# Dropping tokens over capacity: a whole-array copy moved from two DMA queues to one, with the drop test rebuilt on raw semaphores

## The chip, the core and the metric

The kernel runs on one core of one Trainium2 chip. The metric is device time in microseconds (us), lower is better. The time of the kernel before is the median of three runs; beside it stands one profiled execution, which gives the span from the first to the last instruction and everything that is read from the trace. TensorE's granted clock was 1.000 in it.

## What is computed

```python
batch, seq, hidden, capacity = 16, 1024, 512, 256
x = randn(batch, seq, hidden)                            # float32
token_positions = randint(0, capacity, (batch, seq))     # int64 on the device

mask = token_positions < capacity
return x * mask[..., None]
```

There are 16,384 rows of 512 float32 numbers, 2 KB a row and 33.55 MB in all. A row whose position is at or above the capacity becomes zero; any other row is copied. The positions are drawn below the capacity, so with these inputs every row is kept and the output equals x. The kernel doesn't rely on that: it tests the positions while it runs.

## The kernel before, in words

The kernel bets that most rows are kept. It copies all of x to the output from memory to memory, works out a mask meanwhile, and repairs the parts that hold a dropped row.

**The copy (L75).** The rows are seen as 128 groups of 128 neighbouring rows (`(p n) d -> p n d`); a group is 256 KB. The copy is cut along the row in the group into four transfers `k` of 32 rows each (`FIX_COLS`), so that a transfer has 128 pieces of 64 KB, 256 KB apart. Transfers 0 and 2 are issued by SyncE (SP), 1 and 3 by ScalarE (ACT), each with its own DMA queue. They stand at the head of both queues, but for the load of the positions, which SP issues first (L57).

**The mask (L60 to L115).** The positions come as 16 rows of 8 KB. Each is a 64-bit integer, so it is seen as a low and a high 32-bit half: VectorE (DVE) converts `lo` (L81) and `hi` (L82) to float32, makes four comparisons (L86 to L98), and joins them to `f_tile` (L101 to L103): kept if the high half is zero and the low half in 0 to capacity, or if the high half is negative. This mask lies on 16 partitions. To bring it to the 128 partitions of the copy, GpSimd (POOL) builds a selection matrix `e_all` (L60 to L65), and TensorE (PE) multiplies the two in eight steps into `m_psum` (L107), which DVE copies to `m_tile` (L115).

**The flags (L118 to L134).** DVE sums the mask over each of the four parts (`red`), PE sums over the partitions (`s_psum`, L124), and DVE compares with the number of rows in a part: `flag_i` holds four numbers, 1 where a row of the part is dropped. SP, ACT and DVE load all four into registers (L137 and the two lists after it).

**The repair (L153 to L183).** POOL fills two buffers `xt_z` of 8 MB with zeros. For each part u, a load of x into a buffer, 32 multiplications by columns of the mask under a branch on DVE, and a store to the output follow. The load (L163) and the store (L183) are conditional transfers: each is issued in any case and skipped by the value of its flag. The framework's scheduler places the semaphore waits: a store to a part of the output waits until the copy of that part has landed, also when the store is going to be skipped.

```python
eng.dma_start(out=out_r[:, f0 : f0 + FIX_COLS, :], in_=xt,
              cond=eng_flags[eng][u], cond_hint=False)
```

The order on the queues is the order of the code: on SP the positions, copies 0 and 2, loads 0 and 1, stores 1 and 2; on ACT copies 1 and 3, store 0, loads 2 and 3, store 3.

Of the kernel before, what the change touches and what calls it, by code (L numbers as in the profile page):

```python
# [8 lines left out]
@with_exitstack  # L9
def kernel(  # L10
    ctx: ExitStack,
    tc: tile.TileContext,
    x: bass.AP,
    token_positions: bass.AP,
    capacity: bass.AP,
    out: bass.AP,
):
    nc = tc.nc
    P = nc.NUM_PARTITIONS
    fp32 = mybir.dt.float32  # L20
    i32 = mybir.dt.int32

    x_f = x.flatten_outer_dims()
    out_f = out.flatten_outer_dims()
    N, D = x_f.shape
    assert N % P == 0
    n_per_p = N // P

    x_r = x_f.rearrange("(p n) d -> p n d", p=P)
    out_r = out_f.rearrange("(p n) d -> p n d", p=P)  # L30

    tp_f = token_positions.flatten_outer_dims()
    tp_r = tp_f.rearrange("b s -> (b s)") if len(tp_f.shape) == 2 else tp_f
    tp_i32 = tp_r.bitcast(mybir.dt.int32)
    QP = 16
    G = P // QP
    tp_pn = tp_i32.rearrange("(q w) -> q w", q=QP)

    cap = float(int(capacity))

    FIX_COLS = 32
    assert n_per_p % FIX_COLS == 0
    n_fix = n_per_p // FIX_COLS
    rows_per_fix = P * FIX_COLS

    sp = nc.sync
    act = nc.scalar
    hw = (sp, act)

    mask_pool = ctx.enter_context(tc.tile_pool(name="mask", bufs=1))  # L50
    psum_pool = ctx.enter_context(tc.tile_pool(name="psum", bufs=1, space=bass.MemoryType.PSUM))
    NBUF = 2
    io_pool = ctx.enter_context(tc.tile_pool(name="io", bufs=1))

    rows_q = N // QP
    tp_tile = mask_pool.tile([QP, rows_q * 2], i32)
    sp.dma_start(out=tp_tile, in_=tp_pn)  # L57

    e_iota = mask_pool.tile([QP, P], i32, name="e_iota")
    nc.gpsimd.iota(e_iota, pattern=[[1, P]], base=0, channel_multiplier=-G)  # L60
    e_iota_f = mask_pool.tile([QP, P], fp32, name="e_iota_f")
    nc.gpsimd.tensor_copy(out=e_iota_f, in_=e_iota)  # L62
    e_all = mask_pool.tile([QP, G, P], fp32, name="e_all")
    for b in range(G):
        nc.gpsimd.tensor_scalar(  # L65
            out=e_all[:, b, :],
            in0=e_iota_f,
            scalar1=float(b),
            scalar2=None,
            op0=mybir.AluOpType.is_equal,  # L70
        )

    for k in range(n_fix):
        c0 = k * FIX_COLS
        hw[k % 2].dma_start(  # L75
            out=out_r[:, c0 : c0 + FIX_COLS, :], in_=x_r[:, c0 : c0 + FIX_COLS, :]
        )

    lo = mask_pool.tile([QP, G, P], fp32)
    hi = mask_pool.tile([QP, G, P], fp32)  # L80
    nc.vector.tensor_copy(out=lo, in_=tp_tile[:, 0 : 2 * rows_q : 2])  # L81
    nc.vector.tensor_copy(out=hi, in_=tp_tile[:, 1 : 2 * rows_q : 2])  # L82

    f_tile = mask_pool.tile([QP, G, P], fp32)
    t_hi = mask_pool.tile([QP, G, P], fp32)
    nc.vector.tensor_scalar(  # L86
        out=t_hi, in0=hi, scalar1=0.0, scalar2=None, op0=mybir.AluOpType.is_equal
    )
    m2 = mask_pool.tile([QP, G, P], fp32)
    nc.vector.tensor_scalar(  # L90
        out=m2, in0=lo, scalar1=cap, scalar2=None, op0=mybir.AluOpType.is_lt
    )
    m3 = mask_pool.tile([QP, G, P], fp32)
    nc.vector.tensor_scalar(  # L94
        out=m3, in0=lo, scalar1=0.0, scalar2=None, op0=mybir.AluOpType.is_ge
    )
    t_neg = mask_pool.tile([QP, G, P], fp32)
    nc.vector.tensor_scalar(  # L98
        out=t_neg, in0=hi, scalar1=0.0, scalar2=None, op0=mybir.AluOpType.is_lt
    )  # L100
    nc.vector.tensor_tensor(out=f_tile, in0=t_hi, in1=m2, op=mybir.AluOpType.mult)  # L101
    nc.vector.tensor_tensor(out=f_tile, in0=f_tile, in1=m3, op=mybir.AluOpType.mult)  # L102
    nc.vector.tensor_tensor(out=f_tile, in0=f_tile, in1=t_neg, op=mybir.AluOpType.add)  # L103

    m_psum = psum_pool.tile([P, P], fp32, space=bass.MemoryType.PSUM, name="m_psum")
    for b in range(G):
        nc.tensor.matmul(  # L107
            out=m_psum,
            lhsT=e_all[:, b, :],
            rhs=f_tile[:, b, :],  # L110
            start=(b == 0),
            stop=(b == G - 1),
        )
    m_tile = mask_pool.tile([P, n_fix, FIX_COLS], fp32)
    nc.vector.tensor_copy(out=m_tile, in_=m_psum)  # L115

    red = mask_pool.tile([P, n_fix], fp32)
    nc.vector.tensor_reduce(  # L118
        out=red, in_=m_tile, axis=mybir.AxisListType.X, op=mybir.AluOpType.add
    )  # L120
    ones = mask_pool.tile([P, 1], fp32)
    nc.vector.memset(ones, 1.0)  # L122
    s_psum = psum_pool.tile([1, n_fix], fp32, space=bass.MemoryType.PSUM)
    nc.tensor.matmul(out=s_psum, lhsT=ones, rhs=red, start=True, stop=True)  # L124
    flag_f = mask_pool.tile([1, n_fix], fp32)
    nc.vector.tensor_scalar(  # L126
        out=flag_f,
        in0=s_psum,
        scalar1=float(rows_per_fix) - 0.5,
        scalar2=None,  # L130
        op0=mybir.AluOpType.is_lt,
    )
    flag_i = mask_pool.tile([1, n_fix], i32)
    nc.vector.tensor_copy(out=flag_i, in_=flag_f)  # L134

    sp_flags = [
        sp.value_load(flag_i[0:1, u : u + 1], min_val=0, max_val=1)  # L137
        for u in range(n_fix)
    ]
    act_flags = [  # L140
        act.value_load(flag_i[0:1, u : u + 1], min_val=0, max_val=1)
        for u in range(n_fix)
    ]
    ve_flags = [
        nc.vector.value_load(flag_i[0:1, u : u + 1], min_val=0, max_val=1)
        for u in range(n_fix)
    ]
    eng_flags = {sp: sp_flags, act: act_flags}

    xts = []  # L150
    for b in range(NBUF):
        zt = io_pool.tile([P, FIX_COLS, D], fp32, name=f"xt_z{b}")
        nc.gpsimd.memset(zt, 0.0)  # L153
        xts.append(zt)

    ld_eng = {0: sp, 1: sp, 2: act, 3: act}
    st_eng = {0: act, 1: sp, 2: sp, 3: act}

    def emit_load_and_mul(u):
        f0 = u * FIX_COLS  # L160
        xt = xts[u % NBUF]
        eng = ld_eng[u]
        eng.dma_start(  # L163
            out=xt,
            in_=x_r[:, f0 : f0 + FIX_COLS, :],
            cond=eng_flags[eng][u],
            cond_hint=False,
        )
        with tc.If(ve_flags[u]):
            for j in range(FIX_COLS):  # L170
                nc.vector.tensor_scalar(
                    out=xt[:, j, :],
                    in0=xt[:, j, :],
                    scalar1=m_tile[:, u, j : j + 1],
                    scalar2=None,
                    op0=mybir.AluOpType.mult,
                )

    def emit_store(u):
        f0 = u * FIX_COLS  # L180
        xt = xts[u % NBUF]
        eng = st_eng[u]
        eng.dma_start(  # L183
            out=out_r[:, f0 : f0 + FIX_COLS, :],
            in_=xt,
            cond=eng_flags[eng][u],
            cond_hint=False,
        )

    emit_load_and_mul(0)  # L190
    emit_load_and_mul(1)
    emit_store(0)
    emit_store(1)
    emit_load_and_mul(2)
    emit_load_and_mul(3)
    emit_store(2)
    emit_store(3)


# [1 line left out]
_INS = ['x', 'token_positions', 'capacity']  # L201
_OUTS = [((16, 1024, 512), 'float32')]
#: Inputs that are plain numbers.
_NUMBERS = {'capacity': 256}


# [26 lines left out]
```

## Time and profile before

| What | Value |
|---|---|
| median of 3 runs | 106.83 us (106.81 to 107.74) |
| span of the profiled execution | 104.9 us |
| instructions in it | 202 |
| DVE busy | 46.6 us |
| POOL busy | 50.7 us |
| PE busy | 3.9 us |
| bytes moved by DMA packets | 33.69 MB |
| longest DVE instruction (L81, `lo`) | 25.1 us |
| POOL's two zero fills (L153) | 14.0 us each |

The profiled execution has no time of its own beside its span; the median lies 1.9 us above the span. To read the profile: PE is TensorE, DVE VectorE, ACT ScalarE, POOL GpSimd, SP SyncE; a `q` after an engine's name is its instruction queue, which issues transfers and waits. Queue q1 carries SP's transfers and q10 ACT's. The DMA row shows in tenths how busy the 16 DMA engines were in each of 40 slices of the span. In the answers by windows, a row is a stretch of time with each engine's busy time, the clock, the share of the DMA engines and the GB/s; a packet counts in the window in which it starts. The HBM line of the page comes from counters of transfers and not from the packets.

### The profile page before, as it was taken

What the parts mean: (1) busy time and instruction counts of PE and PEld (TensorE: products, weight loads), DVE (VectorE), ACT (ScalarE), POOL (GpSimd) and SP (SyncE); (2) the same over time, 40 slices, a digit from 0 to 9 for tenths busy, and PEclk for the clock granted to TensorE, in tenths of its full rate; (3) what the DMA queues carried; (4) which work ended last, traced back from release to release, by engine and by line L of the source; (5) the groups of instructions that cost most, each with busy time, mean ns of one, the idle gap of its engine ahead of it and who ended that gap; (6) DMA issues with size and microseconds to landing.
All of it is one profiled execution on the core that took longest, in us unless ns stands there. A gap on an engine that the chain in (4) does not pass through costs nothing.

```text
span 104.9 us, 202 instructions
## 1 busy us (share of the span) xinstructions
PE 3.9 (4%) x18; PEld 3.6 (3%) x18; DVE 46.6 (44%) x14; POOL 50.7 (48%) x16
## 2 busy tenths in 40 slices
PE   0000000000000000000940000000000000000000
PEld 0000000000000000000920000000000000000000
DVE  0599999999999999998030000000000000000000
POOL 7999999999999999999600000000000000000000
DMA  9299999909999939999919999759999929999930
GB/s 375 100 375 400 400 400 375 400 25 400 400 400 375 300 125 400 400 400 375 375 50 400 400 400 403 225 175 400 400 400 375 325 100 400 400 400 375 300 125 0
DMA packets 609, 33.69 MB, mean 321 GB/s; under 512 B 80, under 2 KB 80, under 8 KB 80
## 3 DMA queue, kind: packets, MB, share of 16 engines
q1 hardware_dynamic: 320, 16.91, 48.5%
q10 hardware_dynamic: 288, 16.78, 47.4%
q14 instruction: 1, 0.01, 0.0%
HBM read 67.24 MB, written 67.11 MB: 1281 GB/s over the span
## 4 chain that ended last, share of the span: by engine, by line
DVE 44%; PE 4%; DMA 3%; issue 0%
DVE lo L81 24%; DVE m L90 14%; PE m_psum L107 4%; DMA tp_tile<-in_token_positions_dram 3%; DVE f_tile L103 1%; DVE f_tile L102 1%; DVE f_tile L101 1%; DVE m L94 1%; DVE t_neg L98 1%; DVE t_hi L86 1%; DVE hi L82 1%; DVE m_tile L115 0%; DVE red L118 0%; PE s_psum L124 0%; DVE flag_f L126 0%
## 5 line engine op out<-in xcount | busy, mean ns | idle before, releaser
L153 POOL MEMSET xt_z<- 128x16384 f32 x2 | 28.0, 14012 | 0.0
L81 DVE CAST lo<-tp_tile 16x1024 f32<-16x1024 int32 x1 | 25.1, 25121 | 2.9 <-DMA tp_tile<-in_token_positions_dram 2.9
L62 POOL CAST e_iota_f<-e_iota 16x128 f32<-16x128 int32 x1 | 14.3, 14328 | 0.0
L90 DVE TENSOR_SCALAR m<-lo 16x1024 f32<-16x1024 f32 x1 | 14.3, 14305 | 0.0
L65 POOL TENSOR_SCALAR e_all<-e_iota_f 16x128 f32<-16x128 f32 x8 | 8.1, 1023 | 0.3
L107 PE MATMUL m_psum<-f_tile,e_all 16*128 16x128 f32 x16 | 3.8, 424 | 49.6 <-DVE f_tile L103 49.6
L107 PEld LDWEIGHTS m_psum<-f_tile,e_all 16*128 16x128 f32 x16 | 3.5, 326 | 49.6 <-POOL e_all L65 49.6
L115 DVE COPY m_tile<-m_psum 128x128 f32<-128x128 f32 x1 | 0.3, 292 | 3.9 <-PE m_psum L107 3.9
L103 DVE TENSOR_TENSOR f_tile<-f_tile,t_neg 16x1024 f32<-16x1024 f32 x1 | 1.2, 1211 | 0.0
L102 DVE TENSOR_TENSOR f_tile<-f_tile,m 16x1024 f32<-16x1024 f32 x1 | 1.2, 1211 | 0.0
L101 DVE TENSOR_TENSOR f_tile<-t_hi,m 16x1024 f32<-16x1024 f32 x1 | 1.2, 1204 | 0.0
L82 DVE CAST hi<-tp_tile 16x1024 f32<-16x1024 int32 x1 | 0.8, 760 | 0.0
L86 DVE TENSOR_SCALAR t_hi<-hi 16x1024 f32<-16x1024 f32 x1 | 0.8, 759 | 0.0
L94 DVE TENSOR_SCALAR m<-lo 16x1024 f32<-16x1024 f32 x1 | 0.8, 759 | 0.0
L98 DVE TENSOR_SCALAR t_neg<-hi 16x1024 f32<-16x1024 f32 x1 | 0.8, 759 | 0.0
L122 DVE MEMSET ones<- 128x1 f32 x1 | 0.1, 59 | 0.8 <-PEq L214 0.8
L60 POOL IOTA e_iota<- 16x128 int32 x1 | 0.2, 224 | 0.4 <-POOLq L214 0.4
L118 DVE TENSOR_REDUCE red<-m_tile 128x4 f32<-128x128 f32 x1 | 0.3, 286 | 0.0
L126 DVE TENSOR_SCALAR flag_f<-s_psum 1x4 f32<-1x4 f32 x1 | 0.1, 148 | 0.3 <-PE s_psum L124 0.3
L124 PE MATMUL s_psum<-red,ones 128*1 128x4 f32 x2 | 0.2, 166 | 0.7 <-DVE red L118 0.7
L214 POOL MEMSET const-float32-0.0<- 128x1 f32 x1 | 0.1, 98 | 0.2 <-issue 0.2
L134 DVE CAST flag_i<-flag_f 1x4 int32<-1x4 f32 x1 | 0.2, 156 | 0.0
(4 smaller groups left out, 0.4 us busy)
## 6 DMA issues: line engine op xcount, KB each, us to landing
tp_tile<-in_token_positions_dram SPq DMA_DIRECT2D x1, 128.0 KB
out_dram<-in_x_dram ACTq DMA_DIRECT2D x2
out_dram<-in_x_dram SPq DMA_DIRECT2D x2
xt_z<-in_x_dram SPq DMA_DIRECT2D x2
out_dram<-xt_z ACTq DMA_DIRECT2D x2
xt_z<-in_x_dram ACTq DMA_DIRECT2D x2
out_dram<-xt_z SPq DMA_DIRECT2D x2
```

The costliest lines, as they stand in the source:

```text
L62: nc.gpsimd.tensor_copy(out=e_iota_f, in_=e_iota)
L65: nc.gpsimd.tensor_scalar(out=e_all[:, b, :], in0=e_iota_f, scalar1=float(b), scalar2=None, op0=mybir.AluOpType.is_equal,)
L81: nc.vector.tensor_copy(out=lo, in_=tp_tile[:, 0 : 2 * rows_q : 2])
L82: nc.vector.tensor_copy(out=hi, in_=tp_tile[:, 1 : 2 * rows_q : 2])
L86: nc.vector.tensor_scalar(out=t_hi, in0=hi, scalar1=0.0, scalar2=None, op0=mybir.AluOpType.is_equal)
L90: nc.vector.tensor_scalar(out=m2, in0=lo, scalar1=cap, scalar2=None, op0=mybir.AluOpType.is_lt)
L94: nc.vector.tensor_scalar(out=m3, in0=lo, scalar1=0.0, scalar2=None, op0=mybir.AluOpType.is_ge)
L101: nc.vector.tensor_tensor(out=f_tile, in0=t_hi, in1=m2, op=mybir.AluOpType.mult)
L102: nc.vector.tensor_tensor(out=f_tile, in0=f_tile, in1=m3, op=mybir.AluOpType.mult)
L103: nc.vector.tensor_tensor(out=f_tile, in0=f_tile, in1=t_neg, op=mybir.AluOpType.add)
L107: nc.tensor.matmul(out=m_psum, lhsT=e_all[:, b, :], rhs=f_tile[:, b, :], start=(b == 0), stop=(b == G - 1),)
L153: nc.gpsimd.memset(zt, 0.0)
```

## The change

The function's body is written anew inside one critical section, where the scheduler places no waits; seven kinds of raw semaphores order the work.

- The copy is issued by SP alone. x is seen as 16 rows of 2 MB (`(e c) -> e c`), and nine transfers walk along these rows: 64 KB of each row, then 192 KB, then seven times 256 KB. All nine come first on SP's queue.
- The positions are loaded by ACT, as 128 rows of 1 KB, so that the mask lies on 128 partitions from the start. The selection matrix, its matmuls and POOL's part go.
- The mask takes four DVE operations straight on the integer halves (`ge`, `lt`, `low`, `keep`), a sum over the row (`kept`), one matmul over the partitions (`total`) and a comparison, which writes a single flag `drop_i`. Each waits for the one ahead by the semaphore `s_ve`.
- SP, ACT and DVE wait for the flag, load it into a register, and branch once. The repair, inside the branch, handles parts of 16 rows of each group in two buffers with ordinary transfers. ACT waits there for the whole copy before its first store. No zero fill is left.
- At the end SP waits until all nine transfers have landed.

The core of the new code (buffers, semaphores and unused helpers left out; the old code, which is printed above, is removed in full):

```diff
+        x_e = x_b.rearrange("(e c) -> e c", e=16)
+        out_e = out_b.rearrange("(e c) -> e c", e=16)
+        c = 64 * KB
+        at = 0
+        for n in [1, 3] + [4] * 7:
+            sp.dma_start(
+                out=out_e[:, at : at + n * c], in_=x_e[:, at : at + n * c]
+            ).then_inc(s_copy, 16)
+            at += n * c
+            n_copy += 1
...
+        act.dma_start(out=tp, in_=tp_i32.rearrange("(p w) -> p w", p=P)).then_inc(s_tp, 16)
+        lo = tp[:, 0 : 2 * n_per_p : 2]
+        hi = tp[:, 1 : 2 * n_per_p : 2]
...
+        ve.memset(ones, 1.0).then_inc(s_ve, 1)
+        ve.wait_ge(s_tp, 16)
+        ve.tensor_scalar(
+            out=ge, in0=lo, scalar1=0.0, scalar2=None, op0=Alu.is_ge
+        ).then_inc(s_ve, 1)
+        ve.wait_ge(s_ve, 2)
+        ve.scalar_tensor_tensor(
+            out=lt, in0=lo, scalar=cap, in1=ge, op0=Alu.is_lt, op1=Alu.mult
+        ).then_inc(s_ve, 1)
...
+        ve.wait_ge(s_ve, 5)
+        ve.tensor_reduce(
+            out=kept, in_=keep, axis=mybir.AxisListType.X, op=Alu.add
+        ).then_inc(s_ve, 1)
+        pe.wait_ge(s_ve, 6)
+        pe.matmul(out=total, lhsT=ones, rhs=kept, start=True, stop=True).then_inc(s_pe, 1)
+        ve.wait_ge(s_pe, 1)
+        ve.tensor_scalar(
+            out=drop_i, in0=total, scalar1=float(N) - 0.5, scalar2=None, op0=Alu.is_lt
+        ).then_inc(s_ve, 1)
...
+        for e in (sp, act, ve):
+            e.wait_ge(s_ve, 7)
+        ET = mybir.EngineType
+        drop = nc.values_load(
+            drop_i[0:1, 0:1],
+            engines=[ET.SP, ET.Activation, ET.DVE],
...
+        with nc.If(drop):
+            for u in range(n_fix):
+                b = u % NBUF
+                if u >= NBUF:
+                    sp.wait_ge(s_st[b], 16 * (u // NBUF))
+                sp.dma_start(out=xts[b], in_=x_r[:, u * F : (u + 1) * F, :]).then_inc(s_ld[b], 16)
+                ve.wait_ge(s_ld[b], 16 * (u // NBUF + 1))
...
+                if u == 0:
+                    act.wait_ge(s_copy, 16 * n_copy)
+                act.wait_ge(s_mul, (u + 1) * F)
+                act.dma_start(out=out_r[:, u * F : (u + 1) * F, :], in_=xts[b]).then_inc(s_st[b], 16)
...
+        sp.wait_ge(s_copy, 16 * n_copy)
```

## The prediction, made blind

> **What bounds the kernel now.** I read the page's slices and queues first, then the chain of waits, then the queues' own waits and timeline, and last the DMA column of the windows. All durations are of one profiled execution: span 104.9 us. The median of the three timed runs is 106.83, so 1.9 us lie outside the span; I keep them and make the sum as a difference from 106.83.
>
> The page, engines and queues:
>
> ```profile
> PE 3.9 (4%) x18; PEld 3.6 (3%) x18; DVE 46.6 (44%) x14; POOL 50.7 (48%) x16
> ...
> DMA  9299999909999939999919999759999929999930
> ...
> DMA packets 609, 33.69 MB, mean 321 GB/s; under 512 B 80, under 2 KB 80, under 8 KB 80
> ...
> q1 hardware_dynamic: 320, 16.91, 48.5%
> q10 hardware_dynamic: 288, 16.78, 47.4%
> ...
> HBM read 67.24 MB, written 67.11 MB: 1281 GB/s over the span
> ```
>
> The compute engines are idle for more than half of the span; the two queues together fill 95.9% of 16 engines' time. The 33.69 MB are x once (33.55) and the positions (0.13). So no row is dropped and the eight conditional transfers move nothing; the HBM line must count them as if they ran, for it has twice x. The packets can be counted: 80 small ones are 16 completions for each of five transfers. Of the other 528, 512 are the copy (32 per engine, 64 KB each) and 16 are the positions, one row per engine.
>
> The chain of waits ends at the drop flag, not at the kernel's end:
>
> ```profile
> 54.51 0.16 DVE flag_i L134
> ```
>
> The SP queue's own waits, then its timeline:
>
> ```profile
> SPq L137 <- DVE flag_i L134: 52.2, 1, 52.2
> SPq L183 <- DMA out_dram<-in_x_dram: 44.5, 2, 41.7
> ```
>
> ```profile
> 0.74 0.42 SPq L57 DMA_DIRECT2D tp_tile<-in_token_positions_dram  x1
> 1.22 1.26 SPq L75 DMA_DIRECT2D out_dram<-in_x_dram  x2
> 57.42 0.46 SPq L163 DMA_DIRECT2D xt_z<-in_x_dram  x2
> 58.60 45.07 SPq L183 DMA_DIRECT2D out_dram<-xt_z  x2
> ```
>
> The flag is known at 54.7, and SP then waits to about 103.5 for the copy (its last two issues' entry runs to 103.67). So the kernel is one 33.55 MB copy from memory to memory; the flag has 48 us to spare.
>
> The windows tell the pace, because they put a packet's bytes where it starts (the last two columns are DMA share and GB/s):
>
> ```profile
> 2.20:2.30 0.10, 0.00 (x0) 0.00 (x0) 0.00 (x0) 0.10 (x1) 1.00 8.14 2867
> 2.90:5.00 2.10, 0.00 (x0) 0.00 (x0) 1.23 (x1) 2.10 (x1) 1.00 0.00 0
> 5.10:5.20 0.10, 0.00 (x0) 0.00 (x0) 0.10 (x1) 0.10 (x1) 1.00 1.82 655
> 5.80:8.00 2.20, 0.00 (x0) 0.00 (x0) 2.20 (x1) 2.20 (x1) 1.00 0.00 0
> 8.00:8.10 0.10, 0.00 (x0) 0.00 (x0) 0.10 (x1) 0.10 (x1) 1.00 1.86 655
> 11.00:11.10 0.10, 0.00 (x0) 0.00 (x0) 0.10 (x1) 0.10 (x1) 1.00 4.11 1311
> 55.10:55.20 0.10, 0.00 (x0) 0.00 (x0) 0.00 (x0) 0.00 (x0) 1.00 2.09 655
> 64.90:65.00 0.10, 0.00 (x0) 0.00 (x0) 0.00 (x0) 0.00 (x0) 1.00 2.00 737
> 99.10:99.20 0.10, 0.00 (x0) 0.00 (x0) 0.00 (x0) 0.00 (x0) 1.00 2.30 655
> ```
>
> All 16 engines start a 64 KB packet at nearly the same time, then none starts until the next round; the "holes" in the DMA row are this beat against slices of 2.6 us, not idle time. Rounds 0 to 3 start at 2.2, 5.1, 8.0 and 11.0: 8.8 / 3 = 2.93 us each. The last of 32 starts at 99.1: (99.1 - 11.0) / 28 = 3.146 us each after the start. The engines are never idle, so only a faster round makes this kernel faster. A round reads 1.05 MB and writes 1.05 MB: 2.10 MB / 3.146 us = 667 GB/s at the memory, 716 in the first three rounds.
>
> **The change, part by part.**
>
> *Selection matrix, mask arithmetic, memsets of 14.0 us each, conditional transfers: removed.* POOL's 50.7 us and nearly all of DVE's 46.6 go. They all lie beside the copy; gain 0. The new flag: positions by ACT, then five DVE operations of 128 x 128, a one-column matmul and a comparison. By the row of the 128 x 128 copy (292 ns) the five take 1.5 us; even at the longest DVE row here (25.1 us, beside POOL's own slow work) the flag stands before the old one plus the positions' delay. That delay: ACT's eight 1 KB packets per engine may each have to let a 64 KB packet of the copy pass, 8 x 3.1 = 25 us. So the flag comes between 6 and 60 us. The copy covers that to 103; cost 0. If the cover were gone, all of it would count. One value load per engine for four, and one branch not taken: before, 54.7 to 57.4 for the same; hidden too.
>
> *SP's order.* Nine copy issues come first. Before, a 128-row issue took 0.58 to 0.64 us and the 16-row one 0.42, so nine take 3.8 to 5.8 us, over by 6.6 at the latest. The first holds one packet per engine (2.9 us of work), and the second is issued 0.4 to 0.6 us later, so no engine runs dry. Behind SP's new waits stand only its own load, branch and final wait; behind ACT's and DVE's only theirs. If a queue takes fewer descriptors at once (before, each had 18 per engine; now 41), SP stands in an issue, with nothing late behind it.
>
> *Start.* The positions were issued at 0.74 and their packets started from about 1.85; the copy started at 2.2. The copy's first packets should now start at about 1.85: gain up to 0.4. The positions' bytes then run within the copy: the same 0.4 us per engine if bytes count, up to 8 x 0.4 = 3.2 us if each 1 KB packet costs as much as 8 KB did (ten packets in 1.8 to 2.1, by their share 0.38 us each). I take bytes, since semaphore packets of 4 B leave no gap in the rounds. Net 0, from -0.4 to +2.8.
>
> *End.* Before, SP is released at about 103.5 and the span ends at 104.9. A skipped store of 0.1 us goes, the end of the critical section comes; SP's waits at the kernel's own ends sum to 0.6 us. From -0.1 to +0.6; I take 0.
>
> *The copy itself.* This decides. Before, an engine's 32 packets come from two queues and jump by 256 KB; now they are 32 neighbours by address in one 2 MB block, from one queue. Sixteen rows do reach 16 engines: the 16-row positions transfer gave 16 completions. Whether engine and block were differently matched before, the views don't show. No row is this pattern. The nearest rows are both in this trace: 3.146 us per round (two queues mixed), and 2.93 (the first rounds; ACT's transfer was issued 0.48 us before SP's, so these are the ones nearest to one queue in order, but also the ones with an idle memory behind them). I can't part these two reasons, so I take the middle, 3.04: 28 x (3.146 - 3.04) = 3.0 us gained. Ends: 28 x 0.213 = 6.0 gained; and a loss, by the slowest three rounds: rounds 17 and 20 start at 55.1 and 64.9, so 3.27 each; 32 x 3.27 = 104.6 against 8.8 + 29 x 3.146 = 100.0 is +4.6.
>
> Two rules of the Trainium skill bear on that row. First 667 GB/s stands in this trace, 716 at its start; "HBM Reference", Specifications, puts one memory domain at about 716 GB/s. By it the floor for 67.1 MB is 93.7 us of copy, an estimate of some 100.5 us in all, and no pattern gets below. Against the change speaks "DMA: Bandwidth & Descriptors", Latency and other measured facts: copies with rows a large power of two apart lose rate, 164 GB/s at 2 MiB against 214 padded. The engines now stand exactly 2 MiB apart; taken whole, that is an estimate of 100 x 214 / 164 = 130 us of copy, near 137 in all. No run here shows it, and the present pattern is at powers of two as well.
>
> **Sum.** 106.83 + 0 (flag) + 0 (start) + 0 (end) - 3.0 (copy) = 103.8 us.
>
> **The rivals.**
>
> *A. The pace stays.* The memory is the limit, and 64 KB at a time is coarse enough that order doesn't matter. For it: the engines have no gap to lose even with two queues. Against it: 2.93 has been seen. 106.8; with the ends of start and end, 105.8 to 107.9.
>
> *B. The first rounds' pace holds throughout.* 106.83 - 6.0 = 100.8. For it: that is what one queue in order looked like. Against: round 3 already slows while nothing but the mixing and the memory's load changes.
>
> *C. Slower: equal offsets collide.* Each engine now stands at the same offset of its own 2 MB block, reading and writing, so all 32 streams ask the memory for places that differ in high address bits alone. Place: every round. It decides from a round of 3.146 + 1.07 / 32 = 3.18 us; at the slowest rounds' 3.27 the time is 111.4. For it: rounds vary from 2.93 to 3.27 here though bytes are equal, so something other than bytes counts. Against: the engines keep in step already, at equal sizes.
>
> *D. The change doesn't do what it says:* rows of 256 KB are cut otherwise than in 64 KB pieces, or the flag ends last. Then packets would differ in count; the flag would need to be 40 us later than the bounds above. With a pace as before, that is A.
>
> **How the numbers follow.** Forecast's case (rounds of 2.98 to 3.11, 102.0 to 105.8): 0.42. A with D: 0.25. B: 0.09. C: 0.24, half of it beyond 111.0. Faster by over 1% (below 105.8; about what a measurement of this kernel can tell from no change is 1%): 0.42 + 0.09 = 0.51. Within 1%: 0.25. Slower: 0.24. The range 100.6 to 111.0 leaves out 0.12 above and some 0.05 below; the likeliest case's own range is 102.0 to 105.8.
>
> **What would show it.** Page: one queue with 656 packets (512 + 9 x 16) and all the copy's bytes, POOL near 0, DVE under 5 us (right in the removed work). Windows: rounds 3.04 us apart, the first from about 1.85; 3.15 means A, 2.93 B, over 3.18 C. Queue's waits: SP's last one ends within 2 us of the span's end, the flag before 60. I am wrong if the rounds keep their pace, or if gaps open between rounds, against which the queues' 95.9% speaks.

## The result and the profile after

The changed kernel takes 173.32 us (median of 4 runs, 171.91 to 175.29); the kernel before 106.88 beside it. The ratio is 1.614, 95% interval 1.603 to 1.625; it leaves out the changed kernel's slowest run (175.29), which lies more than 1.5% above its fastest. The prediction was 103.8, in a range of 100.6 to 111.0.

The page of the changed kernel, its engines, its DMA row and its queues:

```profile
span 170.1 us, 82 instructions
...
PE 0.2 (0%) x2; PEld 0.1 (0%) x2; DVE 1.6 (1%) x7; POOL 0.2 (0%) x4
...
DMA  9949999879999949999969999979999499999570
...
DMA packets 801, 33.69 MB, mean 198 GB/s; under 512 B 160, under 2 KB 288, under 8 KB 288
...
q1 hardware_dynamic: 656, 33.56, 96.4%
q10 hardware_dynamic: 144, 0.13, 0.2%
...
HBM read 33.69 MB, written 33.55 MB: 395 GB/s over the span
```

Everything that was to go is gone, and the bytes are the same: 656 packets on q1 are the 512 of the copy and 9 x 16 completions. The DMA engines are as full as before (96.6% against 95.9%, both queues together). So the time isn't idle time: each packet takes longer. The share gives how long: 96.4% of 170.1 us x 16 engines over 512 packets is 5.12 us for 64 KB. The same sum for before, 95.9% of 104.9 x 16 / 512, gives 3.14 with the positions in it. This quotient is used below for each run and called its pace. It includes what else the copy's queue carried.

The HBM line, which comes from counters, now agrees with the packets, where before it had twice x. The only transfers that went are the conditional ones, which were skipped; so it had counted them.

The rest of the changed kernel's timeline, in the order of time:

```profile
0.90 0.36 ACTq L90 DMA_DIRECT2D tp<-in_token_positions_dram  x1
0.95 6.37 SPq L82 DMA_DIRECT2D out_dram<-in_x_dram  x9
...
3.03 0.23 DVE L97 TENSOR_SCALAR ge<-tp 128x128 f32<-128x128 int32 x1 [1.95 <-DMA tp<-in_token_positions_dram]
...
4.83 0.15 DVE L119 TENSOR_SCALAR drop_i<-total 1x1 int32<-1x1 f32 x1 [0.28 <-PE total L117]
```

The nine issues take 6.37 us, the positions land at 3.0, and the flag stands at 5.0 us instead of 54.7. SP then waits for the copy; by its queue's own waits:

```profile
SPq L156 <- DMA out_dram<-in_x_dram: 160.6, 1, 160.6
```

The windows of the changed kernel, last two columns DMA share and GB/s:

```profile
5.00:25.00 20.00, 0.00 (x0) 0.00 (x0) 0.00 (x0) 0.00 (x0) 1.00 1.03 210
25.00:65.00 40.00, 0.00 (x0) 0.00 (x0) 0.00 (x0) 0.00 (x0) 1.00 1.01 208
65.00:105.00 40.00, 0.00 (x0) 0.00 (x0) 0.00 (x0) 0.00 (x0) 1.00 0.93 187
105.00:145.00 40.00, 0.00 (x0) 0.00 (x0) 0.00 (x0) 0.00 (x0) 1.00 1.03 213
145.00:165.00 20.00, 0.00 (x0) 0.00 (x0) 0.00 (x0) 0.00 (x0) 1.00 1.00 200
```

The copy is slow from its first microseconds and stays so, at 187 to 213 GB/s in each direction where before had 333 (1.049 MB per 3.146 us). What slows it is there in every stretch of the copy.

The rounds have lost their beat, too. Before, the 16 engines started a round's packets within 0.6 to 1.1 us of each other (5.1 to 5.8, 8.0 to 8.6, the last round 99.1 to 100.2). In windows of half a microsecond the changed kernel's second, third and fourth rounds start from 6.0 to 10.0, 11.0 to 14.5 and 16.5 to 20.0 us: the engines are spread over more than half of a packet's 5.12 us.

### The profile page after: what moved, and what is told of

Same layout as the page of the kernel before. It is cut to its first block, busy times and chain, and to the rows that moved or that the text cites. A ratio compares the mean times of both kernels' runs of the same rounds, so it can differ in the third digit from the quotient of the medians.

```text
span 170.1 us, 82 instructions
## 1 busy us (share of the span) xinstructions
PE 0.2 (0%) x2; PEld 0.1 (0%) x2; DVE 1.6 (1%) x7; POOL 0.2 (0%) x4
## 3 DMA queue, kind: packets, MB, share of 16 engines
q1 hardware_dynamic: 656, 33.56, 96.4%
```

## The experiments

Two theories came first. Theory A: it is the addresses; the 16 engines now stand 2 MB apart at equal offsets, and their requests collide at the memory. Theory Q: it is the queue; one queue can't feed the engines as two did. Every time below is of one run, unless a ratio or a number of runs is given. The kernel before, run beside them, took 108.4 to 108.8 us (106.88 beside the changed kernel above), and so the undisturbed pace is 3.18 in these runs, where the trace of before had 3.14. Edits are against the changed kernel unless said otherwise.

### One queue in the kernel before, two in the changed one

```diff
 # kernel before
-        hw[k % 2].dma_start(
+        sp.dma_start(
```

> The kernel before, with all four copies on SP's queue; nothing else is changed. Theory A (addresses: the changed kernel is slow because its 16 DMA engines stand 2 MB apart at equal offsets): the copy's addresses are those of before, so packets of 64 KB take about 3.1 us and the time is 105 to 109 us. Theory Q (queue: one queue can't keep the engines as fast as two): packets of about 5.1 us, about 170 us.

Measured: 108.59 us, before 108.81. Pace 3.20.

```diff
+        act.dma_start(out=tp, ...)                  # moved ahead of the copy
-        for n in [1, 3] + [4] * 7:
-            sp.dma_start(
+        for i, n in enumerate([1, 3] + [4] * 7):
+            (sp, act)[i % 2].dma_start(
```

> The changed kernel, with its nine transfers issued in turn by SP and ACT (the positions first on ACT); addresses as in the changed kernel. Theory A: packets of about 5.1 us, 168 to 178 us. Theory Q: packets of about 3.1 us, 104 to 109 us.

Measured: 186.40 us (span 184.6). Its queue lines:

```profile
q1 hardware_dynamic: 352, 17.83, 51.0%
q10 hardware_dynamic: 448, 15.86, 46.2%
```

With both shares the pace is 97.2% of 184.6 us x 16 / 512 = 5.6 us. One queue costs before nothing, and a second one doesn't help the changed kernel; it is slower still than with one, and lies above theory A's range as well. Theory Q falls. (Why two queues are worse at this distance wasn't followed up.)

### The distance between engines

```diff
-        x_e = x_b.rearrange("(e c) -> e c", e=16)
+        M = 1                                       # 64 KB apart; 4: 256 KB, 8: 512 KB, 16: 1 MB
+        x_e = x_b.rearrange("(a e b) -> e a b", e=16, b=M * c)
```

The output's view and the slices follow; queue, sizes of the transfers and everything else are kept.

> The changed kernel on its one queue, with another share of x for each engine: the 16 engines stand 64 KB apart, so that a round copies one stretch of 1 MB, and each engine jumps 1 MB from packet to packet. Theory A: packets of 2.9 to 3.2 us, 99 to 108 us. Theory Q: about 170 us as in the changed kernel.

> As the 64 KB variant, but the engines stand 256 KB apart and each copies four neighbouring packets before it jumps 4 MB. Theory A: nearer to before than to the changed kernel, 3.1 to 3.6 us a packet, 104 to 122 us; if only the 2 MB distance collides, as before. Theory Q: about 170 us.

> The changed kernel with engines 1 MB apart: each walks 1 MB in order, then jumps 16 MB. Theory S (equal offsets collide: sixteen engines ask at once for places that differ in the high address bits alone): the distance counts, so 1 MB lies between 256 KB (108.4 us) and 2 MB (173): packets of 3.2 to 4.5 us, 108 to 150 us. Theory W (walking in order through far apart blocks is what is slow, at whatever offsets): near the changed kernel, packets of 4.5 to 5.2 us, 150 to 175 us.

> The changed kernel with engines 512 KB apart. 256 KB gave 108.4 us, 1 MB 135.8, 2 MB 173. If the loss sets in with the distance step by step: between 108 and 136 us, packets of 3.2 to 4.0 us. If there is an edge: either 108 (edge above 512 KB) or near 136.

| engines apart | time, us | pace, us per 64 KB |
|---|---|---|
| 64 KB | 108.64 | 3.18 |
| 256 KB | 108.41 | 3.18 |
| 512 KB | 112.86 | 3.33 |
| 1 MB | 135.76 | 4.03 |
| 2 MB (the change; before 106.88) | 173.32 | 5.12 |

The distance alone, on one queue, moves the pace from 3.18 to 5.12. The loss sets in between 256 and 512 KB and then grows with each doubling; there is no single edge. Two lines carry it, the copy's queue with engines 64 KB apart (span 106.9) and with engines 1 MB apart (span 134.0):

```profile
q1 hardware_dynamic: 656, 33.56, 95.2%
```

```profile
q1 hardware_dynamic: 656, 33.56, 96.3%
```

The table also says how the kernel before must have dealt its rows, which its profile didn't show. Had each engine taken eight neighbouring groups, the engines would have stood 8 x 256 KB = 2 MB apart, and four neighbours would have meant 1 MB; the paces at those distances, 5.12 and 4.03, don't fit 3.14. Engines that take neighbouring groups stand 256 KB apart, and that pace fits. This is argued from the paces; no run showed the dealing itself.

### Is it the equal offset, or the walk through a far block?

Theory S: equal offsets collide (each engine asks for the same place in its own block). Theory W: walking in order through blocks far apart is slow at any offset.

```diff
+        def skewed(ap, t, n):                       # engines 2 MB + 64 KB apart
+            return bass.AP(ap.tensor, ap.offset + t * c, [[33 * c, 16], [1, n * c]])
-        for n in [1, 3] + [4] * 7:
+        for n in [1, 3, 4, 4, 4, 1]:
...
+        # then four transfers fill the gaps, engines 64 KB apart
```

> The changed kernel with engines 2 MB and 64 KB apart for the first 17 of 32 packets of each engine: each still walks in order through its own region, but no two engines have equal offsets in 2 MB. The other 15 packets fill the gaps left, with engines 64 KB apart. Theory S: no collision, packets of about 3.2 us from the start, 106 to 112 us. Theory W: the first 17 packets stay near 5.1 us and only the last 15 take 3.2, so 5 + 17 x 5.1 + 15 x 3.2 = 140 us.

Measured: 109.12 us, pace 3.18. The first half, in which each engine still walks its own far block, in the windows:

```profile
5.00:25.00 20.00, 0.00 (x0) 0.00 (x0) 0.00 (x0) 0.00 (x0) 1.00 1.07 358
25.00:55.00 30.00, 0.00 (x0) 0.00 (x0) 0.00 (x0) 0.00 (x0) 1.00 0.98 321
60.00:105.00 45.00, 0.00 (x0) 0.00 (x0) 0.00 (x0) 0.00 (x0) 1.00 0.95 313
```

The skewed part (up to about 55 us) is no slower than the gaps after it. Theory W falls: one queue and a far block for each engine do no harm by themselves.

Then the smallest skews:

```diff
-            return bass.AP(ap.tensor, ap.offset + t * c, [[33 * c, 16], [1, n * c]])
+            return bass.AP(ap.tensor, ap.offset + t * c, [[S, 16], [1, n * c]])   # S: 2 MB + 4 KB; 2 MB + 16 KB
```

> The changed kernel with engines 2 MB and 4 KB apart for 31 of the 32 packets of each engine; two small transfers fill the gaps. It is one of the smallest edits that takes away the equal offsets. Theory S as the 64 KB skew left it: if 4 KB are enough to part the engines at the memory, packets of about 3.2 us, 107 to 112 us. If the offsets must differ by about as much as a packet, the collision stays: packets of 4 to 5 us, 135 to 173 us.

Measured: 168.78 us, pace 5.01, from its queue's line (span 167.0):

```profile
q1 hardware_dynamic: 928, 33.56, 96.0%
```

The offsets are unequal, and the loss is nearly whole. So theory S in its plain form falls too. The spread of the starts in the changed kernel agrees: the engines don't touch exactly equal offsets at one moment there either.

> The changed kernel with engines 2 MB and 16 KB apart for 28 of 32 packets; small transfers fill the gaps. 4 KB left 5.06 us a packet, 64 KB gave 3.18. Theory E (only exactly equal offsets collide) has fallen with the 4 KB run. Theory R (the loss is set by how far the sixteen engines are spread over the addresses below 2 MB: 4 KB x 15 = 60 KB is too little, 64 KB x 15 = 960 KB is enough): 16 KB x 15 = 240 KB lies between, packets of 3.3 to 4.8 us, 112 to 162 us. If an edge lies below 16 KB: 3.2 us, 108 to 112 us; if above: 5 us, near 168.

Measured: 124.00 us, pace 3.61 (its 240 gap packets of 17 KB counted by their bytes). A step between: the pace goes 5.12, 5.01, 3.61, 3.18 for skews of 0, 4, 16 and 64 KB. The more the engines differ in the addresses below 2 MB, the smaller the loss; 4 KB each is hardly a help, and 16 KB isn't enough. The windows of the 16 KB run show that its value is no mixture of a slow and a fast stretch:

```profile
25.00:65.00 40.00, 0.00 (x0) 0.00 (x0) 0.00 (x0) 0.00 (x0) 1.00 1.00 283
65.00:100.00 35.00, 0.00 (x0) 0.00 (x0) 0.00 (x0) 0.00 (x0) 1.00 0.97 283
```

### Reads or writes?

```diff
-        x_e = x_b.rearrange("(e c) -> e c", e=16)
+        x_e = x_b.rearrange("(e r k) -> e r k", e=16, k=c)      # reads 2 MB apart
-        out_e = out_b.rearrange("(e c) -> e c", e=16)
+        out_e = out_b.rearrange("(r e k) -> e r k", e=16, k=c)  # writes 64 KB apart; the reverse in the other run
```

> Reads of x as in the changed kernel (engines 2 MB apart), writes with engines 64 KB apart, so the rows of the output are permuted. If only the reads collide: packets of about 5.1 us, near 173 us. If only the writes do: about 3.2 us, near 109 us. If both do alike: near 4.2 us, about 140 us. The queue theory has no say any more.

> The reverse: reads with engines 64 KB apart, writes 2 MB apart as in the changed kernel, so the rows of the output are permuted. If only the writes collide: near 173 us. If only the reads do: near 109 us. If both do alike: about 140 us.

In both runs the rows of the output are permuted. Measured: 136.84 us with reads 2 MB apart (span 135.1, pace 4.06), 142.65 with writes 2 MB apart (span 140.9, pace 4.21); their queue lines in this order:

```profile
q1 hardware_dynamic: 656, 33.56, 96.1%
```

```profile
q1 hardware_dynamic: 656, 33.56, 95.5%
```

Each side is slowed by itself, and the two losses add up: 4.06 - 3.18 = 0.88 and 4.21 - 3.18 = 1.03 make 1.91, where both together cost 5.12 - 3.18 = 1.94.

### What the rest of the change is worth

> The 256 KB variant again, with enough rounds to tell one per cent: everything of the change but the 2 MB distance (one queue, no selection matrix, no zero fills, no conditional transfers, one flag). The prediction's steps put each of these at 0: ratio to before 0.99 to 1.01. If the removed work of POOL and DVE or the skipped transfers had held up the copy: below 0.99.

Measured: 108.66 us (median of 12 runs) against 108.60 (17 runs), ratio 1.0005, 95% interval 0.9976 to 1.0035. One queue, the new mask, the one branch, the lost fills and conditional transfers together are worth nothing that this measurement can see.

### What holds the undisturbed pace, and can it be beaten?

```diff
+            sp.dma_start(out=hold[...], in_=x_b[...].rearrange("(p f) -> p f", p=P))   # 4 x 4 MB to SBUF
+        # then the upper 16 MB as in the 64 KB variant
```

> Half of the work changed: the first 16 MB of x are only loaded into SBUF (their output is left out), then the other 16 MB are copied as in the 64 KB variant. It asks what holds a packet of the undisturbed copy at 3.13 us. If reading and writing the same memory at once is the limit (667 GB/s): reads alone run faster, 2.4 us for 64 KB, and then 3.2 for the copy; about 16 x 2.4 + 16 x 3.2 + 6 = 96 us. If the engines or their one queue are: 3.1 us throughout, 108 us.

Measured: 96.33 us; the output of the first 16 MB is not written. Its windows, first while it only reads, then while it copies:

```profile
5.00:25.00 20.00, 0.19 (x2) 0.09 (x2) 1.54 (x6) 0.00 (x0) 1.00 1.02 440
25.00:40.00 15.00, 0.00 (x0) 0.00 (x0) 0.00 (x0) 0.00 (x0) 1.00 0.99 428
55.00:85.00 30.00, 0.00 (x0) 0.00 (x0) 0.00 (x0) 0.00 (x0) 1.00 0.99 321
```

One queue keeps the same engines at about 430 GB/s when they only read the memory (into SBUF, in packets of 32 KB), 2.4 us for 64 KB, and at about 320 when they copy. So neither the engines' reading nor the queue holds the copy at 3.1 to 3.2 us; what holds it comes in with the writes to the memory. Whether the writes alone would be as slow, or only reads and writes together, stays open: no run only writes.

Packets of 16 KB were tried for a faster copy, 16 KB apart in the 64 KB variant's order, and at 256 KB apart with the bytes in the 256 KB variant's order:

```diff
 # 16 KB apart
-        c = 64 * KB
+        c = 16 * KB
-        for n in [1, 3] + [4] * 7:
+        for n in [4, 12] + [16] * 7:
 # 256 KB apart
+                    max_dma_last_dim=16384,
```

> The 64 KB variant with pieces of 16 KB, engines 16 KB apart, in search of a copy that is faster than before: four times as many packets, a round covers 256 KB. If the 3.13 us for 64 KB are the memory's limit whatever the order: 106 to 110 us, ratio 0.99 to 1.02. If wide jumps between packets cost something: 98 to 105 us.

> The 256 KB variant (ratio 1.0005 with packets of 64 KB) with packets of 16 KB in the same order of bytes. It parts the two causes of the 114.3 us of packets of 16 KB at 16 KB distance. Theory R: the distance was too small there (16 KB x 15 = 240 KB), so here packets take a quarter of 3.2 us, 107 to 111 us, ratio 0.99 to 1.02. If a small packet costs time of its own: near 114, ratio 1.05.

Measured: 113.21, 113.45 and twice 115.11 us for the first (pace 3.31 in the run of 113.45), outside both of its expected ranges, and for the second 112.84, ratio 1.0385 (1.0326 to 1.0444; pace 3.30). Neither is faster. The paces agree. The simplest reading is that the small packet costs time of its own, an estimated 0.03 us for each 16 KB packet ((3.30 - 3.18) / 4), and that engines 16 KB apart lose no more than at 256 KB. That speaks against theory R as it was put (the spread of the engines below 2 MB sets the loss): 16 KB x 15 below 2 MB cost a good deal with 2 MB between the engines, and nothing here. It is not the spread alone; what the further address bits add stays open, and so does which bits choose the place in the memory. No variant beat the kernel before.

## Why the prediction was wrong, step by step

- **The copy's pace is the step that failed.** The term was -3.0 us, with ends of -6.0 and +4.6. By the pace the 32 rounds took 32 x 5.12 = 163.8 us instead of 100.0: +63.8 of the 65.2 us by which the two profiled spans differ (the medians differ by 66.4). Of the other 1.4 us, 0.2 is the copy's later start (2.4 against 2.2 us), and at least a part of the rest is one engine that ends behind the others: its last completion starts at 168.4 us, the others' from 164.7 to 167.5. The term's ends came from rows of the kernel before, and by their paces none of those rows had engines 2 MB apart; the table of distances is the row that was missing.
- **Rival C was right that the addresses of the engines slow the copy, and where** ("Place: every round")**, and got its price and its chance wrong.** The price was bounded by the slowest rounds of before, 3.27, which occur while the mean pace is that of harmless distances. Its counterargument, that the engines keep in step already, says nothing of how far apart they stand while they do; and in the changed kernel they no longer keep in step. Its condition, equal offsets, was too narrow: 4 KB of difference left the loss nearly whole. The text noted that the views don't show how engine and block were matched before, and then weighed C as if the match might be the same.
- **The gain was not there.** 2.93 in the first rounds was read half as a sign for one queue in order. The kernel before on one queue has 3.20, and the 256 KB variant on one queue a ratio of 1.0005. In the former the rounds start at 2.6, 5.5, 8.4, 11.5 and 14.7 us and the last at 101.0: two rounds of 2.9, then 3.1, then 3.20 on average, all on the same queue. So the faster start belongs to the first microseconds and not to the number of queues; why it is faster stays open.
- **The terms at 0 were right in sum** (ratio 1.0005 without the 2 MB distance), one of them by another way. The copy was to start at 1.85 with the positions' packets in among it. In the windows of the changed kernel the positions' packets start from 1.8 us on, nearly all of them by 2.4, and the copy's at 2.4: ACT issued 0.05 us ahead of SP, and SP's first issue took 1.02 us against a median of 0.61. So there was no earlier start, and the feared passing of eight copy packets did not arise. q10 holds 0.2% of 170.1 us, 0.3 us per engine, as by bytes.
- **The two rules of the Trainium skill.** "DMA: Bandwidth & Descriptors", Latency and other measured facts, pointed the right way: its 164 GB/s at a row pitch of 2 MiB against 214 for a padded one (which it measured at 4 MiB) made an estimate of 137, and 173 was measured; the prediction named it and left it out of its range. On the cure the runs differ from it: it says that a pad of 4 KiB brings the full rate back (for tiles of 128 rows), while here, with 16 engines each in its own row, 2 MB + 4 KB left 5.01 us of 5.12, 16 KB wasn't enough and 64 KB was. The measurement decides. "HBM Reference", Specifications (716 GB/s for a domain), fits the undisturbed copy (660 GB/s read and written together, 2.10 MB per 3.18 us); the changed kernel's 410 GB/s are far below both.
- **D was out:** 656 packets, sixteen engines, flag at 5.0 us. That is a little before the stated 6 to 60, and SP's nine issues took 6.37 us, over at 7.3, where 3.8 to 5.8 and 6.6 were stated; nothing waited behind either.
- **One range was read wrongly.** Rival A's 105.8 to 107.9 is 1% on either side of 106.83; the stated ends of start and end (-0.4 to +2.8 and -0.1 to +0.6) would give 106.3 to 110.2.

## What to carry to other kernels

When a copy is bound by its transfers, ask of any new view which addresses the 16 engines touch at the same time, not only how neatly each one walks: a distance of 2 MB between them cost 66 us here, while all the compute that the change removes was worth nothing that could be measured. A distance of 64 to 256 KB, or a skew of 64 KB on top of 2 MB, kept the full pace here. A pattern that no row of the trace shows can't be bounded by rows of another pattern; say so, and let the range reach to what a named rival would cost in full.

## What the runs showed of the hardware that was not expected

- Reads 2 MB apart and writes 2 MB apart are each slow by themselves, and the losses add (0.88 + 1.03 against 1.94 us per 64 KB).
- A difference of 4 KB between the engines' offsets is hardly a help at 2 MB (5.01 against 5.12 us), and 16 KB wins back about three quarters of the loss (3.61, undisturbed 3.18).
- Two queues at 2 MB are slower than one: 186.4 against 173.3 us (one run of the first).
- DVE's conversion of 16 x 1024 integers took 25.1 us before, beside POOL's work; in the changed kernel, without POOL, the four mask operations on the same integers as 128 x 128 took 0.23 to 0.29 us each. Neither moved the end.
